# Expert outputs split by engine in runs, their products put off; the first gather evicted ahead of the routing weights; small experts 2nd, 5th and 8th

## Chip, core and metric

One core of a Trainium2 chip runs the whole program. The time is device microseconds of one execution. TensorE is called PE here, VectorE DVE, ScalarE ACT, GpSimd POOL; SP is the queue that issues the weight transfers. TensorE's granted clock is given as a share: 1.00 is its level of 2.4 GHz, 0.50 its level of 1.2 GHz.

## What is computed

A decoder of two layers over 272 tokens (16 of them learned, dropped at the end) and 1024 channels. Each layer has a token mixer; layer 0 then has a dense SwiGLU and layer 1 a mixture of eight experts, two for each token. The change lies in the experts and in the step just ahead of them.

```python
def moe_swiglu(x, router_w, wg, wu, wd):
    xt = x.reshape(-1, d)
    logits = (xt @ router_w).astype(jnp.float32)
    top_v, top_i = lax.top_k(logits, TOP_K)
    top_w = jax.nn.softmax(top_v, axis=-1)
    comb = jnp.sum(jax.nn.one_hot(top_i, N_EXPERTS) * top_w[..., None], axis=1)
    out = jnp.zeros_like(xt)
    for e in range(N_EXPERTS):
        out = out + comb[:, e:e + 1] * swiglu(xt, wg[e], wu[e], wd[e])
...
return rms_norm(h, g_final)[:, N_META:]
```

The widths are 1024 channels, 3584 hidden per expert, 8 experts, float32 throughout.

## The kernel before

Up to about 745 us the program runs the two mixers and the dense layer. At the end of the second mixer `by_tokens` turns the hidden state to tokens by channels and keeps it as a high and a low part (`nh`, `nl`), and forms the router's logits. Then comes the routing: DVE compares logits (L1018 to L1026) to find the two experts of each token, PE counts positions (L1030 to L1034), DVE makes one-hot matrices (`onehot`), and `gather` multiplies them with `nh` and `nl` to collect the tokens of an expert in `xg`. The gather's result lies in PSUM; ACT evicts the even channel blocks (L1098) and DVE the odd ones (L1096). Meanwhile the routing weights `comb` are worked out by a chain of small DVE and ACT steps (L1149 to L1164), and `residual` adds `nh` and `nl` into the accumulators `hacc` on POOL (L1000). POOL then clears four tiles `YD` (L1246).

The eight experts run one after the other (`experts`, loop over q). An expert has room for 96 tokens ("B" in `KINDS`, a big one) or 64 ("S", a small one). The order is set by hand: `RANKS` says which place takes the expert of which rank by number of tokens (expert 0 is always first), and small places take the ranks 5, 6 and 7. The weights of an expert are 42 units of 1 MB. SP issues them in order into a ring of 16 buffers (6 `raw`, 4 more `raw`, 2 more, and the old tiles `xh`, `xl`, `lt`, `mg`); a unit is issued when the buffer of the unit 16 before it is released by PE. From the fourth hidden block of the first expert on, SP first reads the order of the experts from `idxi` (`load_order`, L1423).

An expert has 7 hidden blocks j. For each, `gate_up` forms gate and up (2 units each, `products` with `halves`, L1212, of 64 tokens, and for a big expert also `quarters`, L1217, of the other 32), `hidden` transposes the product (L1312), and `down` (2 units) accumulates into the two output banks `dn_` (tag `t`). Between the two ways of a product (or in the middle of it for a small expert) PE takes work from the list `pending`: two items in the gate product, one in the up product, one in the down product.

At the end of an expert, `results(q, d)` for the two halves d of the channels calls `split_y`, which splits the output bank into a high part (ACT copy, L285) and a low part (DVE subtraction, L286), in six pieces for a big expert and two for a small one, into the `YD` tiles (named `wlo` and `whi` in the profile). Then `scatter(t, d)` multiplies these with the transposed one-hot matrix `oht` (the output product, L1259, 128x512) and DVE adds the weighted result into `hacc` (L1260). These four scatters are items of `pending`. PSUM tags have a fixed number of banks: `BANKS = {"acc": 3, "s": 2, "t": 2, "o": 1}`. Gate and the transposes use `acc`, up uses `s`, and the output products use `o`, of which there is one. By tile dependencies an engine that reads a bank after another engine has read it waits for that one.

Before the last `down` of a group of experts (`GROUPS`) the next group is gathered.

Of the kernel before, what the change touches and what calls it, by code (L numbers as in the profile page):

```python
# [7 lines left out]
F32 = mybir.dt.float32  # L8
F32R = mybir.dt.float32r
BF16 = mybir.dt.bfloat16  # L10
I32 = mybir.dt.int32
AF = mybir.ActivationFunctionType
OP = mybir.AluOpType
# [3 lines left out]
P = 128  # L17
D = 1024
# [17 lines left out]
MORE = CAP - SMALL  # L36
PASSES = -(-(SEQ - SMALL) // CAP)

RANKS = (0, 5, 1, 6, 2, 3, 4, 7)
KINDS = "BSBSBBBS"  # L40
GROUPS = ((0,), (1, 2), (3, 4), (5, 6, 7))
ALLBIG = "B" * 8
PAIRS = ((0, 1), (2, 3), (4, 5), (6, 7))
# [164 lines left out]
def _build(ctx, tc, nc, A, out, dbg):  # L208
    V, S, G, PE = nc.vector, nc.scalar, nc.gpsimd, nc.tensor
# [3 lines left out]
    def units_of(pool, n):  # L213
        return [lambda: pool.tile([P, UNIT], F32, name="raw")] * n
# [26 lines left out]
    def bank(tag):  # L241
        return psum.tile([P, 512], F32, name=tag, bufs=BANKS[tag])
# [8 lines left out]
    st = Stream(nc, w, units_of(rawp, NRAW), hlp, NHL, 0, dbg.get("units", UNITS))  # L251
# [32 lines left out]
    def split_to(hi, lo, src):  # L284
        S.activation(hi, src, AF.Copy)  # L285
        V.tensor_tensor(lo, src, hi.bitcast(F32), op=OP.subtract)  # L286
# [611 lines left out]
    em = {}  # L898
# [57 lines left out]
    def low_part(c):  # L956
        d = slice((c - 1) * P, (c + 1) * P)
        V.tensor_tensor(em["nl"][:, :, d], em["tp"].rearrange("p (t f) -> p t f", t=2),
                        em["nh"][:, :, d].bitcast(F32), op=OP.subtract)
# [31 lines left out]
    def one(shape, dt, nm):  # L991
        return mo.tile(shape, dt, name=nm, bufs=1)

    acc = [[one([P, 512], F32, f"hacc{t}{d}") for d in range(2)] for t in range(2)]

    def residual(d):

        cs = slice(d * 512, (d + 1) * 512)
        for t in range(2):
            G.tensor_tensor(acc[t][d], em["nh"][:, t, cs].bitcast(F32), em["nl"][:, t, cs].bitcast(F32), op=OP.add)  # L1000

    residual(0)
    more = units_of(ctx.enter_context(tc.tile_pool(name="rawc", bufs=NRAWC)), NRAWC)
    st.more(*more)

# [1 line left out]
    me = em["pool"]  # L1007
# [38 lines left out]
    pending = []  # L1046
# [96 lines left out]
    V.tensor_copy(posr[:, :, 0], pos[:, :, 0])  # L1143
    fast = Run(KINDS, GROUPS, posr, combr)
    fast.onehot(0)
    low_part(KD - 1)
    residual(1)

    V.reciprocal(ssq, ssq)  # L1149
    for t in range(2):  # L1150
        V.tensor_scalar(L[:, t, :], L[:, t, :], ssq[:, t:t + 1], None, op0=OP.mult)
    V.tensor_reduce(mx_, L, axis=AX.X, op=OP.max)
    V.tensor_tensor(comb, L, mx_[:, :, None].to_broadcast([P, 2, NEXP]), op=OP.subtract)
    st.advance()
    S.activation(comb, comb, AF.Exp)
    for c2 in range(4):
        fast.gather(0, c2, ("acc", "s")[c2 % 2])
    for n in ("nh", "nl"):
        st.once(lambda: me.tile([P, 2, D], F32R, name=n).rearrange("p t f -> p (t f)").bitcast(F32))
    S.activation(rs, ssq, AF.Silu)  # L1160
    V.tensor_tensor(comb, comb, sel, op=OP.mult)
    V.tensor_reduce(mx_, comb, axis=AX.X, op=OP.add)
    V.reciprocal(mx_, mx_)
    V.tensor_tensor(comb, comb, mx_[:, :, None].to_broadcast([P, 2, NEXP]), op=OP.mult)  # L1164
    ranks = em["ranks"]
    for q, r in enumerate(RANKS):
        G.memset(ranks[:, q:q + 1], float(r))
    pair_ = [em["sqs"][:, i * 64:(i + 1) * 64].rearrange("p (a b) -> p a b", a=NEXP) for i in range(2)]
    quad = em["sqs"][:, 128:].rearrange("p (t a b) -> p t a b", t=2, a=NEXP)
    rank = one([P, NEXP], F32, "rank")  # L1170
# [6 lines left out]
    def rank_steps():  # L1177

        a, b = pair_
        V.tensor_copy(cnr, cn)  # L1180
        V.tensor_scalar(cnr[:, 0:1], cn[:, 0:1], 2.0 * SEQ, None, op0=OP.add)
        cj, ce = cnr[:, None, :].to_broadcast(sq), cnr[:, :, None].to_broadcast(sq)
        V.tensor_tensor(a, cj, ce, op=OP.is_gt)
        V.tensor_tensor(b, cj, ce, op=OP.is_equal)
        V.tensor_tensor(b, b, lower, op=OP.mult)
        yield
        V.tensor_tensor(a, a, b, op=OP.add)
        V.tensor_reduce(rank, a, axis=AX.X, op=OP.add)
        V.tensor_tensor(a, rank[:, None, :].to_broadcast(sq), ranks[:, :, None].to_broadcast(sq), op=OP.is_equal)
        yield  # L1190
        V.tensor_tensor(b, a, em["index"][:, None, :].to_broadcast(sq), op=OP.mult)
        V.tensor_reduce(idx, b, axis=AX.X, op=OP.add)
        V.tensor_copy(idxi, idx)
        yield
        for src, dst in ((pos, posr), (comb, combr)):
            V.tensor_tensor(quad, src[:, :, None, :].to_broadcast([P, 2, NEXP, NEXP]),
                            a[:, None].to_broadcast([P, 2, NEXP, NEXP]), op=OP.mult)
            V.tensor_reduce(dst, quad, axis=AX.X, op=OP.add)
            yield

        V.tensor_scalar(caps, rank, float(NEXP - 1 - KINDS.count("S")), float(-MORE), op0=OP.is_gt, op1=OP.mult)
        V.tensor_scalar(caps, caps, float(CAP), None, op0=OP.add)
        V.tensor_tensor(cnr, cn, caps, op=OP.subtract)
        V.tensor_reduce(cnt, cnr, axis=AX.X, op=OP.max)
        V.tensor_scalar(cnt, cnt, 0.0, None, op0=OP.max)
        V.tensor_copy(cnti, cnt)
        yield
# [33 lines left out]


    YD = [[spare_half(n).rearrange("p (d c) -> p d c", d=2) for n in ns] for ns in (("wlo", "wlo"), ("wlo", "whi"))]
    for pair in YD:
        for y in pair:
            G.memset(y.bitcast(F32), 0.0)  # L1246

    def split_y(run, q, d, a):
        for (hi, lo), n, c0, cw in ((YD[0], SMALL, 0, 256), (YD[1], MORE, 256, P))[:1 if run.small(q) else 2]:
            for i in range(P // n):  # L1250
                r, c = slice(i * n, (i + 1) * n), slice(i * cw, (i + 1) * cw)
                split_to(hi[r, d, c], lo[r, d, c], a[r, c0:c0 + cw])

    def scatter(run, q, oht, t, d, tag):
        p = bank(tag)
        n = 1 if run.small(q) else 2
        for i in range(n):
            for k, y in enumerate(YD[i]):
                PE.matmul(p, lhsT=oht[:, (2 * i + t) * P:(2 * i + t + 1) * P], rhs=y[:, d, :], start=i + k == 0, stop=i + k == n)  # L1259
        V.scalar_tensor_tensor(acc[t][d], p, run.comb[:, t, q:q + 1], acc[t][d], op0=OP.mult, op1=OP.add)  # L1260
# [37 lines left out]
    pending = []  # L1298

    def experts(st, run, first):  # L1300

        hid, dn_, oht = {}, {}, {}
# [54 lines left out]
        def results(q, d, final):  # L1357

            split_y(run, q, d, dn_[q][d])
            pending.extend([lambda t=t: scatter(run, q, oht[q], t, d, "acc" if final else "o") for t in range(2)])  # L1360
            if final:
                pending.append(lambda: square_sums(d))

        for q in range(NEXP):
            final = q == NEXP - 1
            i = run.group[q]
            turnover = q == run.groups[i][-1] and not final
            last = None
            oht[q] = mo.tile([P, 4 * P], F32R, name="oht")
            if q == 0:  # L1370
                pending.append(lambda: run.by_slot(0, oht[0], first))
                if first:
                    ranking = rank_steps()
                    pending.extend([lambda: next(ranking)] * 6)
            for j in range(FJ):
                gate_up(q, j, last)
                last = (q, j)
                if first and q == 0 and j == FJ - 4:
                    load_order()
                    for n in range(4):  # L1380
                        pending.append(lambda n=n: again_by_tokens(n // 2, n % 2))
                if turnover and j == FJ - 2:
                    run.onehot(i + 1)
                if j == 0:
                    continue
                if j == 1:
                    dn_[q] = [bank("t"), bank("t")]
                    if q:
                        pending.append(lambda q=q: run.by_slot(q, oht[q]))

                def between():
                    if j == FJ - 1:
                        hidden(q, j)
                    spare_time(1)

                down(q, j - 1, between)
                if final and j == FJ - 2:
                    pending.extend([lambda d=d: g_final(d) for d in range(2)])
            if turnover:
                for c2 in range(4):  # L1400
                    run.gather(i + 1, c2, ("s", "acc")[c2 % 2])
            if final:
                spare_time(len(pending))
                S.activation(mx_, ssq, AF.Sqrt)
                XG["fin"] = st.spare().rearrange("p (t d f) -> p t d f", t=2, d=2)

            def between():
                if final and run.small(q):
                    results(q, 0, final)

            down(q, FJ - 1, between)
            for d in range(1 if final and run.small(q) else 0, 2):
                results(q, d, final)
# [150 lines left out]
```

## Time and profile before

| what | value |
|---|---|
| median of 3 runs | 1677.03 us (1676.4 to 1677.11) |
| profiled execution, its own time | 1677.67 us |
| its span, from the first instruction to the last | 1676.0 us |
| PE busy | 1621.8 us, 97% of the span |
| DVE, ACT, POOL busy | 618.6, 464.1 and 139.9 us |
| weights' queue q1 | 469.86 MB, 72.0% of 16 engines' time |
| chain that ended last | PE 92%, DVE 2%, ACT 2%, POOL 2% |

A busy time says that an engine had an instruction, not that it ran at full clock. In a timeline row the first number is the start in us from the span's start and the second the length; "x16" is the number of records that were merged (a float32 matmul leaves two), and a bracket gives the idle time of the engine just before and what ended it.

### The profile page before, as it was taken

What the parts mean: (1) busy time and instruction counts of PE and PEld (TensorE: products, weight loads), DVE (VectorE), ACT (ScalarE), POOL (GpSimd) and SP (SyncE); (2) the same over time, 40 slices, a digit from 0 to 9 for tenths busy, and PEclk for the clock granted to TensorE, in tenths of its full rate; (3) what the DMA queues carried; (4) which work ended last, traced back from release to release, by engine and by line L of the source; (5) the groups of instructions that cost most, each with busy time, mean ns of one, the idle gap of its engine ahead of it and who ended that gap; (6) DMA issues with size and microseconds to landing.
All of it is one profiled execution on the core that took longest, in us unless ns stands there. A gap on an engine that the chain in (4) does not pass through costs nothing.

```text
span 1676.0 us, 41156 instructions
## 1 busy us (share of the span) xinstructions
PE 1621.8 (97%) x18303; PEld 1336.7 (80%) x18303; DVE 618.6 (37%) x1120; ACT 464.1 (28%) x811; POOL 139.9 (8%) x210
## 2 busy tenths in 40 slices
PE   8999999999999999998998999989999899999895
PEld 8999999999999999996775667756677677677563
DVE  5667676555556676762112010120101200200202
ACT  5545656444444457541101000010000100100101
POOL 2301342000011012510000000000000000000000
PEclk9999999999999999998999999999999999999998
DMA  7334454544543346477897999999999899899893
GB/s 295 126 127 151 152 176 155 195 171 172 179 174 127 126 151 267 187 276 282 340 378 300 420 418 417 418 403 420 418 418 417 354 368 379 309 369 385 329 419 119
DMA packets 66290, 472.80 MB, mean 282 GB/s; under 512 B 7345, under 2 KB 7473, under 8 KB 9521
## 3 DMA queue, kind: packets, MB, share of 16 engines
q1 hardware_dynamic: 65952, 469.86, 72.0%
q8 instruction: 148, 2.42, 0.6%
q14 instruction: 46, 0.37, 0.1%
q10 hardware_dynamic: 144, 0.15, 0.0%
HBM read 468.93 MB, written 1.05 MB: 280 GB/s over the span
## 4 chain that ended last, share of the span: by engine, by line
PE 92%; DVE 2%; ACT 2%; POOL 2%; issue 1%; DMA 1%; SPq 0%; ACTq 0%; DVEq 0%; POOLq 0%
PE s L1212 12%; PE acc L1212 12%; PE t L1212 12%; PE acc L280 8%; PE acc L282 8%; PE acc L281 8%; PE acc L1217 4%; PE s L1217 4%; PE t L1217 4%; PE s L280 2%; PE s L282 2%; PE s L281 2%; PE t L280 2%; PE t L281 2%; PE t L282 2%; PE o L1259 2%
## 5 line engine op out<-in xcount | busy, mean ns | idle before, releaser
L167 DVE TENSOR_TENSOR wlo<-raw,whi 128x1024 fp32r<-128x1024 f32 x218 | 271.5, 1246 | 36.2 <-PE acc L282 13.6
L154 ACT ACTIVATE whi<-raw 128x1024 fp32r<-128x1024 f32 x218 | 229.3, 1054 | 155.7 <-issue 51.5
L280 PE MATMUL acc<-xh,whi 128*128 128x272 f32 (+1 forms) x864 | 252.8, 293 | 0.0
L282 PE MATMUL acc<-xh,wlo 128*128 128x272 f32 (+1 forms) x864 | 247.9, 287 | 0.8 <-DVE wlo L167 0.8
L281 PE MATMUL acc<-xl,whi 128*128 128x272 f32 (+1 forms) x864 | 247.1, 286 | 0.0
L1313 DVE COPY whi<-acc 128x384 f32<-128x384 f32 (+1 forms) x56 | 28.4, 508 | 500.8 <-PE acc L1312 500.8
L1343 ACT ACTIVATE es<-acc 128x384 f32<-128x384 f32 (+1 forms) x49 | 21.8, 444 | 586.8 <-PE acc L1312 540.1
L1212 PE MATMUL acc<-raw,xg 128*64 128x256 f32 x1328 | 160.3, 393 | 4.3 <-issue 4.3
L280 PEld LDWEIGHTS acc<-xh,whi 128*128 128x128 f32 x864 | 162.7, 188 | 1.6 <-issue 0.9
L282 PEld LDWEIGHTS acc<-xh,wlo 128*128 128x128 f32 x864 | 162.7, 188 | 1.0 <-DVE wlo L167 1.0
L281 PEld LDWEIGHTS acc<-xl,whi 128*128 128x128 f32 x864 | 163.0, 189 | 0.1
L1212 PE MATMUL s<-raw,xg 128*64 128x256 f32 x1344 | 156.9, 381 | 0.0
L1212 PE MATMUL t<-raw,whi 128*64 128x256 f32 x1328 | 152.6, 380 | 0.0
L1212 PEld LDWEIGHTS acc<-raw,xg 128*64 128x64 f32 x1328 | 97.6, 142 | 58.0 <-issue 15.2
L1212 PEld LDWEIGHTS s<-raw,xg 128*64 128x64 f32 x1344 | 93.7, 137 | 50.2 <-issue 5.9
L1212 PEld LDWEIGHTS t<-raw,whi 128*64 128x64 f32 x1328 | 93.7, 137 | 48.5 <-issue 3.1
L1344 DVE TENSOR_TENSOR es<-s,es 128x384 f32<-128x384 f32 (+1 forms) x49 | 24.5, 500 | 96.4 <-PE s L1212 76.6
L280 PE MATMUL t<-xh,whi 128*128 128x272 f32 (+1 forms) x208 | 60.0, 288 | 0.0
L282 PE MATMUL t<-xh,wlo 128*128 128x272 f32 (+1 forms) x208 | 59.9, 288 | 0.0
L281 PE MATMUL t<-xl,whi 128*128 128x272 f32 (+1 forms) x208 | 59.6, 286 | 0.0
L797 POOL TENSOR_TENSOR mg<-mg,g 128x272 f32<-128x272 f32 (+1 forms) x32 | 44.6, 1393 | 106.7 <-DVE g L796 106.7
L1217 PE MATMUL acc<-raw,xg 128*32 128x128 f32 x1696 | 53.0, 275 | 0.0
(457 smaller groups left out, 2704.9 us busy)
## 6 DMA issues: line engine op xcount, KB each, us to landing
raw<-w SPq DMA_DIRECT2D x356, 1024.0 KB, 8.0
xh<-w SPq DMA_DIRECT2D x21, 1024.0 KB, 11.8
xl<-w SPq DMA_DIRECT2D x21, 1024.0 KB, 12.6
lt<-w SPq DMA_DIRECT2D x21, 1024.0 KB, 12.8
mg<-w SPq DMA_DIRECT2D x21, 1024.0 KB, 13.6
raw<-w SPq DMA_DIRECT2D x6, 512.0 KB, 8.6
hT<-hT SPq DMA_DIRECT2D x4, 272.0 KB, 6.8
lw<-lruw SPq DMA_DIRECT2D x2, 512.0 KB, 8.3
```

The lines of the kernel that those rows point to most:

```text
L154: self.nc.scalar.activation(hi, src, AF.Copy)
L167: self.nc.vector.tensor_tensor(lo, src, hi.bitcast(F32), op=OP.subtract)
L280: PE.matmul(ps, lhsT=wh, rhs=xh, start=start, stop=False)
L281: PE.matmul(ps, lhsT=wh, rhs=xl, start=False, stop=False)
L282: PE.matmul(ps, lhsT=wl, rhs=xh, start=False, stop=stop)
L797: G.tensor_tensor(mg[c][:, :NQ], mg[c][:, :NQ], g[:, :NQ], op=OP.add)
L1212: PE.matmul(a[g * SMALL:(g + 1) * SMALL, :256], lhsT=x, rhs=w[:, g * 256:(g + 1) * 256], start=start, stop=stop)
L1217: PE.matmul(a[r * MORE:(r + 1) * MORE, 256:384], lhsT=x, rhs=w[:, r * P:(r + 1) * P], start=start, stop=stop, tile_position=(0, r * MORE))
L1259: PE.matmul(p, lhsT=oht[:, (2 * i + t) * P:(2 * i + t + 1) * P], rhs=y[:, d, :], start=i + k == 0, stop=i + k == n)
L1313: V.tensor_copy(h[1][:, :w], p[:, :w])
L1343: S.activation(s[:, :w], gu[0][:, :w], AF.Silu)
L1344: V.tensor_tensor(s[:, :w], gu[1][:, :w], s[:, :w], op=OP.mult)
```

## The change

1. `KINDS` goes from "BSBSBBBS" to "BSBBSBBS", and `RANKS` with it: the small experts are the 2nd, 5th and 8th.
2. `split_y` makes all ACT copies of a half first, then all DVE subtractions.
3. The output products of a non-final expert are put off by two items of `pending`, and those of t = 1 use a bank of tag `acc` instead of `o`.
4. `gather` for the first expert, with its evictions, stands ahead of the routing weights; `residual` moves from POOL to DVE, behind the routing weights.
5. The clearing of `ranks` and `YD` on POOL moves into the first two of what are now eight steps of `rank_steps`; the call `st.advance()` is left out (no instruction belongs to it here).

```diff
-RANKS = (0, 5, 1, 6, 2, 3, 4, 7)
-KINDS = "BSBSBBBS"
+RANKS = (0, 5, 1, 2, 6, 3, 4, 7)
+KINDS = "BSBBSBBS"
 GROUPS = ((0,), (1, 2), (3, 4), (5, 6, 7))
...
         for t in range(2):
-            G.tensor_tensor(acc[t][d], em["nh"][:, t, cs].bitcast(F32), em["nl"][:, t, cs].bitcast(F32), op=OP.add)
-
-    residual(0)
+            V.tensor_tensor(acc[t][d], em["nh"][:, t, cs].bitcast(F32), em["nl"][:, t, cs].bitcast(F32), op=OP.add)
...
     low_part(KD - 1)
-    residual(1)
+    for c2 in range(4):
+        fast.gather(0, c2, ("acc", "s")[c2 % 2])
 
     V.reciprocal(ssq, ssq)
...
-    st.advance()
     S.activation(comb, comb, AF.Exp)
-    for c2 in range(4):
-        fast.gather(0, c2, ("acc", "s")[c2 % 2])
-    for n in ("nh", "nl"):
-        st.once(lambda: me.tile([P, 2, D], F32R, name=n).rearrange("p t f -> p (t f)").bitcast(F32))
...
+    for d in range(2):
+        residual(d)
+    for n in ("nh", "nl"):
+        st.once(lambda: me.tile([P, 2, D], F32R, name=n).rearrange("p t f -> p (t f)").bitcast(F32))
...
+        for q, r in enumerate(RANKS):
+            G.memset(ranks[:, q:q + 1], float(r))
+        yield
+        for y in YD[0] + YD[1]:
+            G.memset(y.bitcast(F32), 0.0)
+        yield
...
     def split_y(run, q, d, a):
+        parts = []
         for (hi, lo), n, c0, cw in ((YD[0], SMALL, 0, 256), (YD[1], MORE, 256, P))[:1 if run.small(q) else 2]:
             for i in range(P // n):
                 r, c = slice(i * n, (i + 1) * n), slice(i * cw, (i + 1) * cw)
-                split_to(hi[r, d, c], lo[r, d, c], a[r, c0:c0 + cw])
+                parts.append((hi[r, d, c], lo[r, d, c], a[r, c0:c0 + cw]))
+        for hi, lo, src in parts:
+            S.activation(hi, src, AF.Copy)
+        for hi, lo, src in parts:
+            V.tensor_tensor(lo, src, hi.bitcast(F32), op=OP.subtract)
...
             split_y(run, q, d, dn_[q][d])
-            pending.extend([lambda t=t: scatter(run, q, oht[q], t, d, "acc" if final else "o") for t in range(2)])
+            if not final and d == 0:
+                pending.extend([lambda: None] * 2)
+            pending.extend([lambda t=t: scatter(run, q, oht[q], t, d, "acc" if final or t else "o") for t in range(2)])
...
-                    pending.extend([lambda: next(ranking)] * 6)
+                    pending.extend([lambda: next(ranking)] * 8)
```

On PE the end of the first expert (big) and the beginning of the second (small) stood like this before; `t` is the expert's output bank, `acc` and `s` with `xg` are gate and up of the next expert, and L1259 are the output products:

```order
L1217 MATMUL t<-xh,whi 32x128 x16
L1212 MATMUL acc<-xl,xg_10143 64x256 x8
L1259 MATMUL o<-wlo,oht 128x512 x3
L1259 MATMUL o<-whi,oht 128x512
L1259 MATMUL o<-wlo,oht 128x512 x3
L1259 MATMUL o<-whi,oht 128x512
L1212 MATMUL acc<-lt,xg_10143 64x256 x8
L1212 MATMUL s<-mg,xg_10143 64x256 x8
L1259 MATMUL o<-wlo,oht 128x512 x3
L1259 MATMUL o<-whi,oht 128x512
```

And so in the changed kernel, where the output products are L1264 and the products L1215 and L1220:

```order
L1220 MATMUL t<-xh,whi 32x128 x16
L1215 MATMUL acc<-xl,xg_10143 64x256 x8
L1215 MATMUL acc<-lt,xg_10143 64x256 x8
L1215 MATMUL s<-mg,xg_10143 64x256 x8
L1264 MATMUL o<-wlo,oht 128x512 x3
L1264 MATMUL o<-whi,oht 128x512
L1215 MATMUL s<-raw,xg_10143 64x256 x8
L1215 MATMUL acc<-raw,xg_10143 64x256 x8
L1264 MATMUL acc<-wlo,oht 128x512 x3
L1264 MATMUL acc<-whi,oht 128x512
L1264 MATMUL o<-wlo,oht 128x512 x3
L1264 MATMUL o<-whi,oht 128x512
```

The first output product now stands behind three stretches of eight matmul pairs instead of one, and the second one has a bank of its own and two more such stretches ahead of it.

On ACT, at the same place, the six copies of each half of the output (d = 0, then d = 1) stood before with these waits:

```order
L285 ACTIVATE wlo<-t 64x256 [waits PE_49,Pool_49]
L285 ACTIVATE wlo<-t 64x256 [waits DVE_49]
L285 ACTIVATE wlo<-t 32x128 [waits DVE_49,Pool_49]
L285 ACTIVATE wlo<-t 32x128 [waits DVE_49] x3
L285 ACTIVATE wlo<-t 64x256 [waits PE_49]
L285 ACTIVATE wlo<-t 64x256 [waits DVE_49]
L285 ACTIVATE wlo<-t 32x128 [waits DVE_49] x4
```

and in the changed kernel:

```order
L1255 ACTIVATE wlo<-t 64x256 [waits PE_49,Pool_49]
L1255 ACTIVATE wlo<-t 64x256
L1255 ACTIVATE wlo<-t 32x128 [waits Pool_49]
L1255 ACTIVATE wlo<-t 32x128 x3
L1255 ACTIVATE wlo<-t 64x256 [waits PE_49]
L1255 ACTIVATE wlo<-t 64x256
L1255 ACTIVATE wlo<-t 32x128 x4
```

The waits of a copy for DVE's subtraction of the piece before are gone; DVE waits once for each half instead.

On DVE, between the routing and the first expert, this piece of the difference begins behind the last low part (L958); L1149 to L1153 are the first steps of the routing weights, L1096 (now L1095) the evictions of the gather:

```order
 L958 TENSOR_TENSOR nl<-o,nh 128x2x256
+L1095 TENSOR_SCALAR xg_8853<-acc,par 128x96
+L1095 TENSOR_SCALAR xg_8853<-s,par 128x96
+L1095 TENSOR_SCALAR xg_8853<-acc,par 128x96
+L1095 TENSOR_SCALAR xg_8853<-s,par 128x96
 L1149 RECIPROCAL ssq<-ssq 128x2
 L1151 TENSOR_SCALAR L<-L,ssq 128x8 x2
 L1152 TENSOR_REDUCE mx<-L 128x2
 L1153 TENSOR_TENSOR comb<-L,mx 128x16
-L1096 TENSOR_SCALAR xg_8863<-acc,par 128x96
-L1096 TENSOR_SCALAR xg_8863<-s,par 128x96
-L1096 TENSOR_SCALAR xg_8863<-acc,par 128x96
```

A little further on DVE, behind the routing weights (L1159) and ahead of the one-hot matrix of the first expert's output (L1105, on which PE's transposes wait), the changed kernel has:

```order
L1159 TENSOR_TENSOR comb<-comb,mx 128x16
L1000 TENSOR_TENSOR hacc_8782<-nh,nl 128x512
L1000 TENSOR_TENSOR hacc_8784<-nh,nl 128x512
L1000 TENSOR_TENSOR hacc_8783<-nh,nl 128x512
L1000 TENSOR_TENSOR hacc_8785<-nh,nl 128x512
L1105 TENSOR_SCALAR whi<-wide,posr 128x256 x2
```

So the evictions have moved ahead of four small steps, and four additions that were POOL's now stand ahead of the one-hot matrix.

## Rows read from the trace of the kernel before

**Rows 1.** Waits of PE from 730 us on: us in total, times, longest.

```profile
PE o L1259 <- DVE hacc L1260: 21.0, 7, 4.2
PE acc L1212 <- issue: 4.3, 1, 4.3
PE o L1259 <- ACT wlo L285: 2.9, 4, 0.9
PE acc L1030 <- DVE selb L1025: 1.0, 1, 1.0
```

**Rows 2.** Timeline at the ends of the first and the sixth expert, PE, ACT and DVE.

```profile
882.74 0.38 ACT L285 ACTIVATE wlo<-t 64x256 fp32r<-64x256 f32 x1 [4.31 <-PE t L1217]
...
883.42 1.95 PE L1212 MATMUL acc<-xl,xg 128*64 128x256 f32 x16
...
883.67 0.38 ACT L285 ACTIVATE wlo<-t 64x256 fp32r<-64x256 f32 x1 [0.55 <-DVE wlo L286]
...
891.03 0.75 DVE L1260 SCALAR_TENSOR_TENSOR hacc<-o,combr,hacc 128x512 f32<-128x512 f32 x1
...
891.84 1.65 PE L1259 MATMUL o<-wlo,oht 128*128 128x512 f32 x3 [4.10 <-DVE hacc L1260]
...
1446.26 1.00 PE L1259 MATMUL o<-wlo,oht 128*128 128x512 f32 x3 [2.70 <-DVE hacc L1260]
```

**Rows 3.** Windows behind the five ends of big experts: engines' busy time, PEclk, DMA.

```profile
891.80:897.50 5.70, 5.66 (x22) 3.31 (x24) 0.75 (x1) 0.00 (x0) 0.00 (x0) 0.50 0.00 1
1105.10:1109.10 4.00, 3.95 (x14) 2.35 (x16) 0.75 (x1) 0.00 (x0) 0.00 (x0) 0.50 1.01 422
1318.30:1324.10 5.80, 5.71 (x22) 3.35 (x24) 0.79 (x2) 0.00 (x0) 0.00 (x0) 0.50 0.62 260
1447.00:1450.40 3.40, 3.40 (x57) 2.61 (x58) 0.75 (x1) 0.00 (x0) 0.00 (x0) 0.51 0.00 0
1572.10:1576.70 4.60, 4.54 (x16) 2.65 (x18) 0.76 (x2) 0.00 (x0) 0.00 (x0) 0.50 0.13 53
```

**Rows 4.** Timeline of DVE, POOL and PE around the first gather, and one of DVE's later.

```profile
746.47 1.49 DVE L1018 TENSOR_TENSOR es<-L 128x128 f32<-128x128 f32 x1
747.88 0.28 DVE L1019 TENSOR_TENSOR es<-L 128x128 f32<-128x128 f32 x1
...
751.28 6.34 DVE L1151 TENSOR_SCALAR L<-L,ssq 128x8 f32<-128x8 f32 x2
...
758.62 0.32 DVE L1096 TENSOR_SCALAR xg<-acc,par 128x96 f32<-128x96 f32 x1 [0.51 <-ACT xg L1098]
...
819.69 2.06 DVE L1128 SCALAR_TENSOR_TENSOR nl<-hacc,ssq,nh 128x512 fp32r<-128x512 f32 x3
...
745.25 2.56 POOL L1000 TENSOR_TENSOR hacc<-nh,nl 128x512 f32<-128x512 f32 x2 [25.16 <-PE s L282]
...
756.65 0.95 POOL L1246 MEMSET whi<- 128x1024 f32 x1
...
758.69 6.48 PE L1212 MATMUL acc<-raw,xg 128*64 128x256 f32 x32 [4.26 <-issue]
765.09 0.66 PE L1110 MATMUL o<-ident,whi 128*128 128x128 f32 x4
```

**Rows 5.** Windows in a small expert and in a later big one (columns as in Rows 3).

```profile
920.00:940.00 20.00, 20.00 (x182) 13.01 (x182) 1.70 (x4) 0.77 (x2) 0.00 (x0) 1.00 1.01 418
...
1360.00:1380.00 20.00, 20.00 (x375) 14.91 (x371) 1.67 (x3) 0.49 (x1) 0.00 (x0) 1.00 0.99 378
```

**Rows 6.** Chain that ended last, two pieces one hidden block apart in the first small expert.

```profile
922.43 3.45 PE t L1212 x32
...
933.31 3.45 PE t L1212 x32
```

**Rows 7.** DMA issues: tiles, count, KB each, median us from issue to landing.

```profile
raw<-w SPq DMA_DIRECT2D x356, 1024.0 KB, 8.0
```

**Rows 8.** SP reading the experts' order: count, ns min/median/max, first and last start.

```profile
L1423 SPq TENSOR_LOAD <-idxi x7: 266/273/466, 819.4 to 821.5; - x7
```

More of the change, by code (lines that the diff above doesn't have):

```diff
@@ L1164, in _build @@
     V.tensor_tensor(comb, comb, mx_[:, :, None].to_broadcast([P, 2, NEXP]), op=OP.mult)
+    for d in range(2):
+        residual(d)
+    for n in ("nh", "nl"):
+        st.once(lambda: me.tile([P, 2, D], F32R, name=n).rearrange("p t f -> p (t f)").bitcast(F32))
     ranks = em["ranks"]
-    for q, r in enumerate(RANKS):
-        G.memset(ranks[:, q:q + 1], float(r))
     pair_ = [em["sqs"][:, i * 64:(i + 1) * 64].rearrange("p (a b) -> p a b", a=NEXP) for i in range(2)]
@@ L1243, in _build @@
     YD = [[spare_half(n).rearrange("p (d c) -> p d c", d=2) for n in ns] for ns in (("wlo", "wlo"), ("wlo", "whi"))]
-    for pair in YD:
-        for y in pair:
-            G.memset(y.bitcast(F32), 0.0)
     def split_y(run, q, d, a):
+        parts = []
         for (hi, lo), n, c0, cw in ((YD[0], SMALL, 0, 256), (YD[1], MORE, 256, P))[:1 if run.small(q) else 2]:
```

## The prediction

> **What bounds the kernel now.** PE is busy 97% of the span, so I looked for what it waits for, and then for stretches in which it is busy at half clock. The view of PE's waits from 730 us on [rows 1] names few: 21.0 us in seven waits of an output product for DVE's addition into `hacc`, 2.9 us in four waits for ACT's split, 4.3 us at the first product of the first expert, 1.0 us in the routing. No wait for weights is among them. Every expert but the last has one of the seven: five big ones, of up to 4.2 us, and two small ones.
>
> The timeline at the end of the first expert [rows 2] shows how one comes about. The split runs from 882.74 to 891.03, over 8 us for twelve pieces, because each ACT copy waits for the subtraction before it: 0.38 us of work, 0.55 us of waiting. DVE has both halves' subtractions ahead of the addition L1260, so that starts at 891.03 only, and the second output product, which needs the one bank `o`, at 891.84 after 4.10 us of idle time. At the sixth expert the same wait was 2.70 us.
>
> Then comes the second price: the granted clock. In five stretches behind the big ends [rows 3] PE is busy throughout at 0.50.
>
> The start of the experts has its own delay [rows 4]. DVE's L1018 took 1.49 us, its like L1019 0.28; two L1151 on 8 columns took 6.34 us. Both end as POOL's work ends: L1018 at 747.96 with POOL's `residual` at 747.81, L1151 at 757.62 with the last clearing at 757.60. The gather's evictions stand behind L1151, hence PE's wait of 4.26 us, and the first product then takes 6.48 us, most of it at half clock.
>
> **Output products and splits.** What the change removes at the ends: the 21.0 and 2.9 us of waits [rows 1], and the half-clock stretches. These sum to 5.7 + 4.0 + 5.8 + 3.4 + 4.6 = 23.5 us [rows 3]; at full clock the same work takes half, so 11.7 us go. Together 35.6 us.
>
> Does the new order hide them? At the first end, the six ACT copies of d = 0 start at 882.7 as before and have no wait between them: two of 0.38 us and four that I bound by the same 0.38 make at most 2.3 us. DVE's six subtractions follow, which at 0.43 us each (a bound: the whole alternation is 8.3 us for 12 pairs, 0.69 a pair, copy included) are done by 887.7, those of d = 1 by 890.3. The first output product now stands behind three stretches of 16 records from 883.42 on, each 1.95 us long and some 1.8 us from the next: it comes at about 889, with 1.3 us to spare after its pieces even in these bounds. The second one writes a bank of `acc`, two stretches later; the third needs `o` again, whose addition, 0.75 us of DVE, had some 5 us by then. For a big expert next, the distances are longer. What covers the split is thus gate and up of the next expert; if that cover failed, the price would again be a wait of up to 4.2 us and its half-clock stretch, some 7 us for each big end. What is late next is nothing that I can find: the fourth product needs the `acc` bank of the second, whose addition is over 5 us old.
>
> The two empty items delay only products; the transposed one-hot matrix of the next expert still comes in the down product of its second block. The tail keeps its order, with waits of 0.3 us that I leave.
>
> **The start.** Without `residual` on POOL, L1018 takes 0.28 instead of 1.49 us; PE's wait of 1.0 us for the selection goes, and no more, since PE fills clock up to there. POOL's clearings now wait only for the last readers of their buffers; the last two run from about 745.2 to 747.1 (0.95 us each). If they hold L1018 until 747.1, 0.7 us is gained; I take 1.0, since they end where L1018 has barely begun. The Trainium skill, SBUF — State Buffer, section "Who interferes with whom", says that a DVE instruction with two SBUF inputs contends with a POOL instruction that reads SBUF, not with one that only writes it. A clearing only writes, so by that rule the whole 1.0 us comes; L1018 beside `residual`, which reads, agrees.
>
> The gathers then end at 753.4 instead of 754.4, and their evictions no longer stand behind L1151: the 4.26 us go, and the product starts at 753.5. But PE is not free for long. Its next work, the transposes L1110 (765.09 before), waits for DVE's one-hot matrix, and ahead of that DVE has the last eviction (until 754.4), ten small steps of the routing weights (some 2.2 us with ACT's step between), and now four additions of 128x512. Three similar ones took 2.06 us [rows 4], so 2.75 us for four: 759.4, and with 0.3 us for the one-hot matrix 759.7. PE gets there at 757.1 at full clock or 760.0 at half (3.6 or 6.5 us after 753.5). So the transposes start near 759.9, and the start gains 765.1 - 759.9 = 5.2 us; a new wait of up to 2.6 us takes half of the product's gain. Bounds: 6.0 us if the additions take 0.5 us each; 2 us if the clock falls in the new wait and the next 3.4 to 6.8 us run at half clock.
>
> On that fall the rows leave both open: a wait of 4.10 us and one of 2.70 were followed by half clock [rows 2, 3], and a shorter one, as it would be here, has no row. The Trainium skill, TensorE: Matmul & The Clock Gate, section "HAM oscillation — how this bites in real kernels", says that idle gaps between bursts of matmuls send the clock back to its low level, again at every gap. It speaks against the change only here, where a gap is new, and would take 1.7 us or more from the 5.2.
>
> **The order of the experts.** It moves no work, only the lead of the weights. A unit of 1,048,576 bytes takes 2.51 us at 418 GB/s, the rate with SP always ahead, and 2.77 us at 378, where units come as PE frees buffers in a big expert [rows 5]. A small expert takes 10.88 us for 6 units, 1.81 each [rows 6]. So a small expert shortens the lead by 0.70 x 42 = 29 us and a big one lengthens it by up to 11, its gather and the output products of the expert ahead by some 9 more (an estimate, from their places in the timeline). A full ring is 16 x 2.77 us less the 8.0 us of a landing [rows 7], 36 us. After the first small expert the lead is thus about 7 to 12, as before. With one big expert between two small ones, and its pause of 7 us gone, it would reach only some 27, and the second small expert would end with -2 to 3 us: PE would wait. With two big ones it is full again, and the later two small experts end near 10. I cost this edit at nothing; its cover is a lead of some 7 us at the end of each small expert, and each us beyond it would cost one.
>
> **Sum.** 35.6 + 5.2 = 40.8 us. The profiled execution took 1677.67 us, so 1636.9; the median of the runs shown is 0.6 lower, which makes 1636.
>
> **Rivals.**
> *Weights become the limit.* For it: from the first small expert on, weights come at their highest rate, and PE gets faster. Against: no wait for weights before, and nothing new is consumed faster than a small expert did already. If the lead is misjudged by 10 us at two small ends, 5 to 15 us are lost: 1641 to 1651.
> *The products wait anew.* Bank `acc` now also carries two output products per expert, and DVE's additions queue behind the product of gate and up, which waits for PE. If each of seven ends kept 1 to 3 us of such waits, 7 to 21 us come back: 1643 to 1657.
> *The split stays slow.* If ACT's copies went no faster without their waits, the split would still take 8 us and the first product, now 3.7 us later, would meet no wait, the third perhaps one of 1 to 2 us at five ends: 1641 to 1646.
> *Slower.* SP reads `idxi` before it can issue the rest of the weights, at 819.4 [rows 8], and the steps that make `idxi` now come two items later. All weights would stand still behind it. Two items are some 8 us, and I expect `idxi` well before 819. It decides only from a delay past 819 by the lead of 30 us plus the gain of 41: `idxi` after 890 us makes the kernel slower, by 1 us for each us; at 910 it gives some 1697. A wait of over 6 us in place of each of the seven would do the same, and the longest in the trace is 4.2.
>
> **How the numbers follow.** The forecast, with its own range of 1631 to 1641 (the start's bounds, half a us for each end), has 0.77; weights 0.08; products waiting anew 0.07; split slow 0.03; no change 0.02, if the waits only move to other places; slower 0.03. About 0.2% or 3.4 us is what a measurement of this kernel can tell from no change. Faster is 0.95. The range from 1631 to 1645 takes in the forecast and about half of the two larger rivals.
>
> **What would show it.** PE's waits for `hacc` and for the split gone from its list; no window of clock 0.50 between 770 and 1640; the twelve pieces of a split within 5 to 6 us, copies back to back; the first product near 753.5 and a wait at the transposes for DVE's one-hot matrix, at 759 to 760; 418 GB/s through the first two small experts without a wait of PE for `raw`. Wrong it would be if a wait of more than 1 us stood at each expert's end, or a stretch of 0.50 behind the transposes of the first expert.

## The result, and the profile after

The changed kernel takes 1632.66 us (median of four runs, 1631.08 to 1633.61); the kernel before, run beside it, 1676.72. The ratio is 0.9737, with a 95% interval of 0.972 to 0.9754. The prediction was 1636 us, in a range of 1631 to 1645. The profiled execution, the fastest of the four, took 1631.08 us, with a span of 1629.3; PE is busy for 98% of it.

First the view of PE's waits from 730 us on, after (us in total, times, longest); it answers to [rows 1]:

```profile
PE o L1109 <- DVE whi L1105: 1.8, 1, 1.8
PE o L1115 <- ACT oht L1110: 0.7, 1, 0.7
PE acc L1264 <- DVE wlo L1257: 0.4, 1, 0.4
PE acc L1264 <- DVE hacc L1265: 0.3, 1, 0.3
```

Nothing is left at the seven ends: the first two lines belong to the start of the first expert, the last two to the tail, and before had waits of 0.3 us there too. Next, one window over the seven later experts, from the gate of the second to PE's last product of weights, first of before, then of after (length, busy time of PE, of its weight load, DVE, ACT, POOL; PEclk, DMA share, GB/s):

```profile
883.40:1655.30 771.90, 747.55 (x10409) 522.54 (x10405) 102.43 (x228) 51.93 (x135) 0.00 (x0) 0.98 0.95 382
```

```profile
878.60:1609.70 731.10, 731.10 (x10411) 516.15 (x10405) 102.27 (x228) 51.72 (x135) 0.00 (x0) 1.00 0.99 404
```

The stretch is 40.8 us shorter: 24.35 us of idle time went to nothing, and the busy time fell by 16.45 us. Most of that is the clock, which is at 1.00 throughout, where [rows 3] had 0.50 in five pieces; what the rest is comes below. The weights now come at 404 GB/s on the mean, not far from the 418 of [rows 5].

The timeline at the end of the first expert, which answers to [rows 2]:

```profile
877.97 3.84 ACT L1255 ACTIVATE wlo<-t 64x256 fp32r<-64x256 f32 x12 [4.31 <-PE t L1220]
878.65 1.95 PE L1215 MATMUL acc<-xl,xg 128*64 128x256 f32 x16
879.99 0.86 DVE L1257 TENSOR_TENSOR wlo<-t,wlo 64x256 fp32r<-64x256 f32 x2 [5.91 <-ACT wlo L1255]
880.43 1.90 PE L1215 MATMUL acc<-lt,xg 128*64 128x256 f32 x16
880.88 1.19 DVE L1257 TENSOR_TENSOR whi<-t,wlo 32x128 fp32r<-32x128 f32 x4
...
882.97 1.19 DVE L1257 TENSOR_TENSOR whi<-t,wlo 32x128 fp32r<-32x128 f32 x4
883.98 0.96 PE L1264 MATMUL o<-wlo,oht 128*128 128x512 f32 x3
...
885.22 0.75 DVE L1265 SCALAR_TENSOR_TENSOR hacc<-o,combr,hacc 128x512 f32<-128x512 f32 x1 [1.07 <-PE o L1264]
...
889.75 0.86 PE L1264 MATMUL o<-wlo,oht 128*128 128x512 f32 x3
```

ACT's twelve copies stand back to back in 3.84 us, and the split is done at 884.16, 6.2 us after it began (8.3 before). None of PE's rows here has a bracket, that is, PE waits for nothing: the pieces of d = 0 are ready at 882.07, the first product comes at 883.98; its addition ends at 885.97, the bank `o` is needed again at 889.75.

The start of the experts, which answers to [rows 4]:

```profile
745.86 0.95 POOL L1181 MEMSET whi<- 128x1024 f32 x1
...
746.27 0.29 DVE L1017 TENSOR_TENSOR es<-L 128x128 f32<-128x128 f32 x1
...
753.03 3.67 PE L1215 MATMUL acc<-raw,xg 128*64 128x256 f32 x32
...
755.70 2.49 DVE L1000 TENSOR_TENSOR hacc<-nh,nl 128x512 f32<-128x512 f32 x4
...
758.51 0.81 PE L1109 MATMUL o<-ident,whi 128*128 128x128 f32 x4 [1.81 <-DVE whi L1105]
...
760.99 3.54 PE L1220 MATMUL acc<-raw,xg 128*32 128x128 f32 x64
```

The product starts at 753.03 without a wait and runs at full clock, the transposes come 6.6 us earlier than before, and behind their wait the clock fell: the 64 records of L1220 take 3.54 us, in other runs of this place 1.96.

### The profile page after: what moved, and what is told of

It is laid out like the page before. It is cut to its first block, busy times and chain, and to the rows that moved or that the text cites. A ratio compares the mean times of both kernels' runs of the same rounds, so it can differ in the third digit from the quotient of the medians.

```text
span 1629.3 us, 41145 instructions
## 1 busy us (share of the span) xinstructions
PE 1604.1 (98%) x18303; PEld 1330.5 (82%) x18303; DVE 614.5 (38%) x1124; ACT 464.4 (29%) x811; POOL 135.4 (8%) x206
## 4 chain that ended last, share of the span: by engine, by line
PE 95%; POOL 1%; DVE 1%; DMA 1%; ACT 1%; issue 0%; ACTq 0%; DVEq 0%; POOLq 0%
PE s L1215 12%; PE t L1215 12%; PE acc L1215 12%; PE acc L280 8%; PE acc L282 8%; PE acc L281 8%; PE acc L1220 4%; PE t L1220 4%; PE s L1220 4%; PE s L280 2%; PE s L281 2%; PE s L282 2%; PE t L280 2%; PE t L281 2%; PE t L282 2%; PE acc L1317 2%
## 5 line engine op out<-in xcount | busy, mean ns | idle before, releaser
L1215 PE MATMUL s<-raw,xg 128*64 128x256 f32 x1344 | 156.8, 381 | 0.0
L1215 PE MATMUL t<-raw,whi 128*64 128x256 f32 x1328 | 153.1, 381 | 0.0
L1215 PE MATMUL acc<-raw,xg 128*64 128x256 f32 x1328 | 152.5, 380 | 0.0
L1215 PEld LDWEIGHTS s<-raw,xg 128*64 128x64 f32 x1344 | 93.8, 137 | 50.6 <-issue 6.6
L1215 PEld LDWEIGHTS acc<-raw,xg 128*64 128x64 f32 x1328 | 94.2, 137 | 49.1 <-issue 3.2
L1215 PEld LDWEIGHTS t<-raw,whi 128*64 128x64 f32 x1328 | 93.5, 137 | 48.6 <-issue 3.5
L1220 PE MATMUL acc<-raw,xg 128*32 128x128 f32 x1760 | 55.9, 279 | 0.0
L1220 PE MATMUL s<-raw,xg 128*32 128x128 f32 x1760 | 54.2, 274 | 0.0
```

The source lines that it names most:

```text
L1215: PE.matmul(a[g * SMALL:(g + 1) * SMALL, :256], lhsT=x, rhs=w[:, g * 256:(g + 1) * 256], start=start, stop=stop)
L1220: PE.matmul(a[r * MORE:(r + 1) * MORE, 256:384], lhsT=x, rhs=w[:, r * P:(r + 1) * P], start=start, stop=stop, tile_position=(0, r * MORE))
```

## The experiments

Each kernel differs from before or from the changed kernel in the piece shown. The ratio is to the kernel before on the same chip in the same runs (medians 1676.11, 1676.25 and 1675.24 us for the three groups).

| kernel | median us | ratio, 95% interval |
|---|---|---|
| before + split in runs | 1661.47 | 0.9929 (0.9906 to 0.9953) |
| before + products put off, second bank | 1642.47 | 0.9808 (0.978 to 0.9835) |
| before + start | 1672.12 | 0.9977 (0.9965 to 0.9989) |
| before + order | 1676.12 | 1.0008 (0.9994 to 1.0021) |
| changed, old order | 1638.22 | 0.977 (0.9754 to 0.9787) |
| changed, split as before | 1632.03 | 0.974 (0.9724 to 0.9757) |
| changed, no empty items | 1636.84 | 0.9765 (0.9748 to 0.9781) |
| changed, one bank | 1639.69 | 0.9782 (0.9766 to 0.9799) |
| changed, again | 1630.34 | 0.9739 (0.9717 to 0.9761) |
| changed, residual behind the one-hot matrix | 1628.42 | 0.9731 (0.9708 to 0.9753) |
| changed, residual on POOL | 1630.53 | 0.9748 (0.9725 to 0.9771) |

**One part of the change alone, on the kernel before.** The split in runs:

```diff
+        parts = []
...
-                split_to(hi[r, d, c], lo[r, d, c], a[r, c0:c0 + cw])
+                parts.append((hi[r, d, c], lo[r, d, c], a[r, c0:c0 + cw]))
+        for hi, lo, src in parts:
+            S.activation(hi, src, AF.Copy)
+        for hi, lo, src in parts:
+            V.tensor_tensor(lo, src, hi.bitcast(F32), op=OP.subtract)
```

> The kernel before with the splits in runs alone: all ACT copies of a half, then all DVE subtractions. Theory A (the prediction's): the split of a big end takes 6.2 instead of 8.3 us, but the addition of the first product still stands behind the subtractions of both halves, and the second product still needs the one bank. So each of the five long waits of 2.7 to 4.2 us becomes some 2 us shorter and stays; some 10 us are gained if the half clock stays behind them, up to 20 if it goes where the wait is short: 1657 to 1667 us. Rival B: the slow split is the whole cause, and the products' places and banks matter little: 1636 to 1642 us, with no wait of PE for the addition of over 0.5 us left.

It took 1661.47 us (1655.66 to 1665.08), as theory A says. PE at the first end in its timeline:

```profile
878.75 1.17 PE L1264 MATMUL o<-wlo,oht 128*128 128x512 f32 x3
880.43 0.47 PE L1264 MATMUL o<-whi,oht 128*128 128x512 f32 x1 [0.51 <-DVE whi L1257]
883.21 1.65 PE L1264 MATMUL o<-wlo,oht 128*128 128x512 f32 x3 [2.31 <-DVE hacc L1265]
```

The second product still waits for the addition, 2.31 instead of 4.10 us, and runs at half clock behind it. PE's waits for the addition sum to 12.0 us in seven. The fast split shortens the wait and does not remove it.

Not all of what the profiled execution gains is the edit's. The code of the start is that of before, but in this execution (1655.66 us, the fastest of five) it ran otherwise:

```profile
751.34 2.55 DVE L1151 TENSOR_SCALAR L<-L,ssq 128x8 f32<-128x8 f32 x2
...
754.95 3.67 PE L1212 MATMUL acc<-raw,xg 128*64 128x256 f32 x32 [0.53 <-issue]
```

The two L1151 end at 753.89, with POOL's two additions (753.86), and not with the clearings that follow until 757.65; before it was 6.34 us and the end of the clearings [rows 4]. So the first product starts 3.7 us earlier and at full clock, and the second expert's gate at 876.87, 6.55 us ahead of before. Over the seven later experts this execution takes 757.60 us, where before took 771.90: these 14.3 us are the split's. Two of the twenty runs of before beside it (1668.26 and 1669.38) lie 7 to 8 us under their median; that they began in the same way would fit, and no profile shows it.

The products put off, on a second bank:

```diff
-            pending.extend([lambda t=t: scatter(run, q, oht[q], t, d, "acc" if final else "o") for t in range(2)])
+            if not final and d == 0:
+                pending.extend([lambda: None] * 2)
+            pending.extend([lambda t=t: scatter(run, q, oht[q], t, d, "acc" if final or t else "o") for t in range(2)])
```

> The kernel before with the output products put off by two items and those of t = 1 on a bank of acc, the split as before. Theory A: a split of 8.3 us still ends before the addition of the first product is needed, since the third product comes some 11.8 us behind the first copy; no wait of PE is left at the big ends and no half clock behind them: a gain of 36 to 41 us, 1636 to 1641 us. Rival B (the split must be short): its subtractions of d = 1 end 8.3 us behind the first copy, the first product's addition only after them, and waits of 1 to 3 us with half clock behind them stay at five ends: 1645 to 1660 us.

1642.47 us: most of the gain, but between the theories. No wait at an end is left, so theory A is right about the slow split. What is new are waits for weights, 0.6 us at most and 3.4 in all, and the second small expert, from its first gate product to that of the next expert, takes 86.1 us where the first one takes 81.1. That is the old order, which this kernel still has.

The start (the parts 4 and 5 of the change, as in the diff above):

> The kernel before with the changed start alone: gather ahead of the routing weights, residual on DVE behind them, clearing in the ranking steps. Theory A: the first output products' ends stay as before, the first product of the first expert starts 5.5 us earlier, the transposes behind it wait 1.8 us and the clock falls once: a gain of 4.5 to 5.2 us, 1671.5 to 1672.2 us. Rival B: the starts of experts carry over in full (5.6 us and 1.0 us more): 1670 us or less. Rival C: part of the gain is taken back at the end of the first expert, whose weights' lead is shorter: 1674 to 1676 us.

1672.12 us (1669.62 to 1673.38), theory A. Three rows of PE, the first of them the end of the gathers:

```profile
753.06 0.62 PE L1089 MATMUL s<-oh,nl 128*128 128x96 f32 x2
...
753.61 4.95 PE L1215 MATMUL acc<-raw,xg 128*64 128x256 f32 x32
...
759.09 0.81 PE L1109 MATMUL o<-ident,whi 128*128 128x128 f32 x4 [0.53 <-DVE whi L1105]
```

Here the clock fell during the gathers instead (the last pair takes 0.62 us, most others 0.39), the product took 4.95 instead of 3.67 us, and so the wait behind it was 0.53 instead of 1.81. The transposes come at about the same time either way.

The order:

```diff
-RANKS = (0, 5, 1, 6, 2, 3, 4, 7)
-KINDS = "BSBSBBBS"
+RANKS = (0, 5, 1, 2, 6, 3, 4, 7)
+KINDS = "BSBBSBBS"
```

> The kernel before with the new order of the experts alone. Theory A: the order only moves the lead of the weights, and PE waits for no weight in either order; five ends of big experts cost the same in any order: 1676.7 us, within 1.5. Rival B: it brings part of the 44 us itself, because the old order has its shortest lead (3.2 us) behind the second small expert: 1660 to 1673 us.

1676.12 us, no difference from before: theory A.

**One part undone in the changed kernel.** The old order (the diff just shown, backwards):

> The changed kernel with the old order of the experts (small ones 2nd, 4th and 8th). Theory A (the lead of the weights): without the pauses at the ends the lead is used up in the second small expert; PE waits for raw there and at the beginning of the next big one, 4 to 7 us in all, as in the run with the products put off alone, where that expert took 86.1 us and the first small one 81.1: 1636.5 to 1640 us. Rival B: the order has no part in it, and the time is that of the changed kernel: 1632.7 us, within 1.5.

1638.22 us, theory A. Of its waits of PE those for weights, and then the windows of the first small expert, of the second, and behind it:

```profile
PE t L1215 <- DMA raw<-w: 1.3, 3, 0.6
...
PE acc L1215 <- DMA raw<-w: 0.6, 1, 0.6
...
PE s L1215 <- DMA raw<-w: 0.6, 1, 0.6
PE acc L1215 <- DMA xh<-w: 0.5, 1, 0.5
...
PE s L1220 <- DMA lt<-w: 0.3, 1, 0.3
```

```profile
879.60:960.80 81.20, 81.20 (x710) 51.80 (x707) 13.96 (x34) 6.88 (x21) 0.00 (x0) 1.00 1.01 415
1083.20:1169.10 85.90, 82.56 (x708) 51.81 (x705) 14.17 (x34) 7.34 (x23) 0.00 (x0) 1.00 1.01 419
1169.10:1190.00 20.90, 20.17 (x359) 14.62 (x359) 3.56 (x6) 0.73 (x2) 0.00 (x0) 1.00 1.01 419
```

Weights come at 419 GB/s throughout the second small expert, and PE idles for 3.3 us of it at full clock, all but 0.6 us in waits for weights: there the weights are the limit. The order of the experts is worth nothing in the old kernel and 5.6 us (1638.22 - 1632.66) in the new one.

The split as before (the first diff, backwards):

> The changed kernel with the splits alternating between ACT and DVE as before. Theory A: the products are far enough behind a split of 8.3 us (d = 0 is ready some 4.2 us behind the first copy and needed 6 us behind it; the addition of the first product ends some 9.1 us behind it, and the bank is needed again at 11.8): no wait of PE, 1632.7 us, within 1.5. Rival B: with the slow split waits of 0.5 to 2 us come back at the five big ends, with half clock behind some: 1636 to 1645 us.

1632.03 us: theory A. With the products put off, the split in runs brings nothing that could be measured. The timeline at the first end shows why (last subtraction of d = 0, the first product, the last subtraction of all, the addition, the next use of `o`):

```profile
880.16 0.30 DVE L286 TENSOR_TENSOR whi<-t,wlo 32x128 fp32r<-32x128 f32 x1 [0.34 <-ACT wlo L285]
...
882.09 0.96 PE L1259 MATMUL o<-wlo,oht 128*128 128x512 f32 x3
...
884.04 0.30 DVE L286 TENSOR_TENSOR whi<-t,wlo 32x128 fp32r<-32x128 f32 x1 [0.34 <-ACT wlo L285]
...
884.37 0.75 DVE L1260 SCALAR_TENSOR_TENSOR hacc<-o,combr,hacc 128x512 f32<-128x512 f32 x1
...
887.86 0.86 PE L1259 MATMUL o<-wlo,oht 128*128 128x512 f32 x3
```

Without the empty items:

```diff
-            if not final and d == 0:
-                pending.extend([lambda: None] * 2)
```

> The changed kernel without the two empty items, so that the products come as early as before, those of t = 1 still on a bank of acc. Theory A: the first product stands some 2.6 us behind the first copy, and its pieces are ready at 4.1 us; the third stands at 6 us and the addition it needs ends at 7: 1.5 and 1 us of wait at each of five big ends, with up to 3 us for half clock behind them: 1645 to 1657 us. Rival B: the second bank alone does it: 1632.7 to 1636 us.

1636.84 us, 4.2 more than the changed kernel, below theory A and just above B. I had the third product at 6 us behind the first copy; it stands at 9.2, where its bank is long free. The first product does meet the split, by the list of waits at three of the ends; the list's line, the first of these ends, and the window over the seven experts:

```profile
PE o L1264 <- DVE whi L1257: 1.5, 3, 0.5
```

```profile
882.02 1.18 PE L1264 MATMUL o<-wlo,oht 128*128 128x512 f32 x3
883.71 0.47 PE L1264 MATMUL o<-whi,oht 128*128 128x512 f32 x1 [0.51 <-DVE whi L1257]
884.01 0.86 PE L1264 MATMUL acc<-wlo,oht 128*128 128x512 f32 x3
```

```profile
880.10:1616.10 736.00, 734.52 (x10410) 515.67 (x10405) 102.03 (x228) 51.82 (x135) 0.00 (x0) 1.00 0.99 401
```

From 882.02 to 884.01 the product takes 1.99 us, in the changed kernel 1.13 (883.98 to 885.11). Of these 0.86 us more only 0.51 stand in a bracket; the rest is inside rows that count as busy. The clock stayed up.

One bank:

```diff
-            pending.extend([lambda t=t: scatter(run, q, oht[q], t, d, "acc" if final or t else "o") for t in range(2)])
+            pending.extend([lambda t=t: scatter(run, q, oht[q], t, d, "acc" if final else "o") for t in range(2)])
```

> The changed kernel with all output products but the last expert's on the one bank o again, put off as changed. Theory A: the third product stands directly behind the second and needs the bank whose addition takes 0.75 us behind it: about 1.1 us of wait at each of seven ends, 8 us: 1640 to 1644 us if the clock stays up behind so short a wait, up to 1655 if it falls. Rival B: putting off is enough, the second bank does nothing: 1632.7 us, within 1.5.

1639.69 us, theory A: one wait for the addition at each of seven ends, the clock stays up.

```profile
PE o L1264 <- DVE hacc L1265: 6.5, 7, 0.9
```

```profile
878.40:1617.70 739.30, 732.75 (x10409) 516.91 (x10405) 102.48 (x228) 51.76 (x135) 0.00 (x0) 1.00 0.98 399
```

The window over the seven experts, at full clock, is 8.2 us longer than after's: 6.5 us of idle time and 1.7 us of busy time. A wait costs a quarter of a us more than its bracket says.

**The start once more.** The changed kernel again, beside two variants:

> The changed kernel again, unchanged, beside the two runs that alter its start by a few us: 1632.7 us, within 1.5, and a granted clock of 0.50 somewhere in the 15 us behind the first gather.

1630.34 us (1629.04 to 1633.6).

```diff
-    for d in range(2):
-        residual(d)
...
                 pending.append(lambda: run.by_slot(0, oht[0], first))
+                if q == 0 and first:
+                    pending.append(late_residual)
```

`late_residual` holds the lines taken out above, with the two units that follow them.

> The changed kernel with the four additions of residual on DVE behind the one-hot matrix of the first expert's output, as an item of pending of their own. Theory A: the transposes start 2.5 us earlier and wait for nothing, so 1.8 us are gained for sure, and 1.7 more if the clock then stays up behind the first product: 1629.2 to 1630.9 us. Rival B: the gain is given back, because the additions now hold what comes next on DVE (the copy of rs and the ranking steps), or because the two units that take the place of nh and nl land later: 1632 to 1636 us.

1628.42 us, the lowest median of all, but its interval lies over that of the changed kernel, so a gain is not shown. The wait of 1.81 us is gone from the list, and the clock fell all the same, during the gathers (their last pairs take 0.60 and 0.62 us):

```profile
753.30 4.88 PE L1218 MATMUL acc<-raw,xg 128*64 128x256 f32 x32
...
758.11 0.65 PE L1109 MATMUL o<-ident,whi 128*128 128x128 f32 x4
```

Theory A is right about the wait; the transposes came 0.4 us earlier than in the changed kernel's first profile, not 2.5, since the product ran at half clock.

```diff
-            V.tensor_tensor(acc[t][d], em["nh"][:, t, cs].bitcast(F32), em["nl"][:, t, cs].bitcast(F32), op=OP.add)
+            G.tensor_tensor(acc[t][d], em["nh"][:, t, cs].bitcast(F32), em["nl"][:, t, cs].bitcast(F32), op=OP.add)
```

> The changed kernel with the four additions of residual on POOL again, at their new place behind the routing weights. Theory A: POOL takes 1.28 us for each, 5.1 us from about 755.7 on, and what DVE does beside them with SBUF operands is held as L1018 and L1151 were before; so the one-hot matrix is there at about 761 only, 2.5 us later than now: 1634 to 1637 us. Rival B: an instruction of DVE with one SBUF operand and a scalar is not held, the one-hot matrix is there at 756.5 and PE waits for nothing: 1629 to 1631 us.

1630.53 us, no difference from the changed kernel, and by neither theory's way. POOL has little to do and takes up `residual` as soon as its inputs are there, first at 745.27, far ahead of the place where it stands in the code:

```profile
745.27 2.56 POOL L1000 TENSOR_TENSOR hacc<-nh,nl 128x512 f32<-128x512 f32 x2 [25.19 <-PE s L282]
...
746.50 1.48 DVE L1017 TENSOR_TENSOR es<-L 128x128 f32<-128x128 f32 x1
...
754.01 2.73 POOL L1181 MEMSET wlo<- 128x1024 f32 x3
...
755.22 2.45 DVE L1151 TENSOR_SCALAR L<-L,ssq 128x8 f32<-128x8 f32 x2
...
756.68 0.95 POOL L1181 MEMSET whi<- 128x1024 f32 x1
```

So L1017 is held again (1.48 us, and PE waits 1.0 us for the selection), and L1151 takes 2.45 us for two where the changed kernel has 0.36: it ends at 757.67, with the last clearing at 757.63. The one-hot matrix comes at 759.07 to 759.68. What POOL takes off DVE it gives back by holding it.

## Why the prediction was right

**The mechanism held, place by place.** The waits for `hacc` and the split left PE's list, the half clock left the seven ends, and the gathers' evictions freed the product at 753.03 (753.5 was predicted). The profiled execution is 46.6 us shorter: 4.8 up to the second expert's gate (883.42 to 878.65), 40.8 over the seven later experts, 1.0 in the tail. The prediction had 5.2, 35.6 and nothing. The tail's 1.0 is no gain that is shown: behind the last product of weights the changed kernel's two profiles took 19.6 and 21.2 us, that of before 20.7. One sign was off by little: the twelve pieces of a split took 6.2 us, not 5 to 6.

**The mis-sized term is the price of the waits, 23.9 us.** Idle time of that size went: 24.35 us. But the busy time fell by 16.45 us, not by 11.7. The half clock does not account for the 4.7 us between them: windows cut where the clock itself changes hold 5.69 + 4.00 + 5.80 + 3.41 + 4.62 = 23.5 us of busy time, which is the prediction's sum, and nowhere else over the seven experts is PE busy at 0.50. What the prediction did was to take a bracket for the whole price of a wait, and other kernels show that it isn't. In the one-bank kernel seven waits at full clock brought 1.7 us of busy time beside 6.5 us of idle time. The kernel without empty items has 734.52 us of busy time in its 736.00, against 731.10, at full clock too: 3.4 us beside 1.5 us of idle time. The kernel with the split alone has 743.01 us; its four half-clock stretches, 13.2 us long in busy time, make 6.6 of the 11.9 us that it has more, and 5.3 us stand beside its 14.6 us of idle time. The 4.7 us beside before's 24.35 are of the same kind. That they arise in the same places is argued from the likeness of the ends, not shown. A part can be read in the rows: a stretch of 16 records is listed with 1.95 us and the next one starts 1.78 us later (878.65 and 880.43), so a pause that is counted from the end of such a row is 0.17 us short.

**The start.** The transposes came at 758.51 instead of 759.9: the additions took 0.62 us each, not 0.69, the evictions were done at 753.83, not 754.4. The wait for the one-hot matrix was there (1.81 us; up to 2.6 was predicted). Then the fall of the clock, which stood in the bounds and not in the forecast, took 1.7 us back, so the clause on a half-clock stretch behind the first transposes did come true, with a price inside the range. The start alone measured 4.0 us by the medians. The Trainium skill, TensorE: Matmul & The Clock Gate, section "HAM oscillation — how this bites in real kernels", says that waits between bursts of matmuls, where they are long enough, send the clock back. The traces agree in part: of the six profiles with this wait of 1.8 us the clock fell near it in five, and the seven waits of 0.9 us were followed by no fall.

The Trainium skill, SBUF — State Buffer, section "Who interferes with whom", let a clearing run beside the selection at no cost, and the trace agrees: L1017 takes 0.29 us beside the clearing at 745.86. The same section says that a `tensor_scalar` can enter a mode with two ports in which DVE and POOL block each other, and L1151 beside clearings (2.45 us, alone 0.36) agrees. It does not happen each time: in three of the four profiles with the old start L1151 lasted 6.3 us, until the clearings ended, but with the split alone it ended with the additions, and the transposes came at 758.55 in the old code, as early as in the changed kernel. So what the new start takes away is a delay that varies from one execution to the next, and its 4.0 us are a difference of medians.

**The order at nothing.** Right, and for the reason given: alone it changes nothing, and without it the second small expert of the changed kernel waits for weights. The lead itself was taken too large: 7 to 12 us were predicted behind the first small expert, and the shortest, from a unit's landing to its first use, was 3.5 us, around 966 us.

**The rivals.** Weights as the limit: only with the old order. Products waiting anew: the bank `acc` has waits in the tail alone. The split stays slow: it was priced at 1641 to 1646, and the run with the slow split took 1632.03; the addition that the third product needs ends at 885.12, and the product stands at 887.86, so this rival had no price. Slower by `idxi`: SP read it earlier, not later:

```profile
L1430 SPq TENSOR_LOAD <-idxi x7: 261/267/464, 814.7 to 816.8; - x7
```

**How the parts add up.** Alone, split, products, start and order gain 14.6, 33.6, 4.0 and 0.0 us, together 52.2, where the change gains 44. Split and products shorten the same waits, so the split's 14.6 (14.3 over the seven experts of its profile) are counted twice; the order adds what the products lose to the weights. Within the products, both halves are needed: without the empty items 4.2 us come back, without the second bank 7.0.

## What to carry to other kernels

A wait between engines can be shortened (a faster split) or given distance (a later consumer, a second buffer); where the consumer has other work to do, distance removes it whole, and the shortening is then worth nothing. Before a stall is removed, ask what it gave time to: here the pauses refilled the weights' lead, and the order of the experts had to change with them, an edit that measures as nothing on its own. And price a wait on TensorE above its bracket: the rows around it count part of it as busy, and what runs at half clock behind it comes on top.

## What was not expected

The half clock at the first expert comes and goes with no change in the code there. The windows from 750 to 775 us of three kernels that have the same instructions up to that point (the changed kernel, the same again, and the one with the split as before):

```profile
750.00:775.00 25.00, 22.50 (x324) 17.84 (x327) 8.06 (x30) 5.38 (x12) 0.00 (x0) 0.93 0.74 279
```

```profile
750.00:775.00 25.00, 22.51 (x290) 17.34 (x293) 8.05 (x30) 5.13 (x12) 0.00 (x0) 0.86 0.69 258
```

```profile
750.00:775.00 25.00, 22.50 (x390) 17.72 (x389) 8.07 (x30) 5.15 (x12) 0.00 (x0) 1.00 0.75 302
```

The mean clock is 0.93, 0.86 and 1.00, and the three executions took 1631.08, 1633.6 and 1629.59 us: the order is the same. From the selection (L1017, at 746.27, 746.01 and 746.04) to the second expert's gate (878.65, 879.57 and 876.76) they take 132.4, 133.6 and 130.7 us, so the half clock costs 1.7 and 2.8 us here. Of the 4.0 us between the slowest and the fastest, 1.2 come from the tail instead (21.2 against 20.0 us behind the last product of weights); the seven experts take 731.1, 731.1 and 731.0. What decides where the clock falls remains open: it also fell where the wait had been taken away.
